# A conformer/RWKV-7 layer on one core: lora weights in buffers of their own, zero parts of tiles that persist, the first convolution tap and the bias on VectorE, and samples that write the output page

## The chip, the cores and the metric

The kernel runs on one core of a Trainium2 chip. The time is device microseconds of one execution of the whole program. Below, PE is the matrix engine (TensorE) and PEld its weight loads, DVE is VectorE, ACT is ScalarE, POOL is GpSimd and SP is the engine whose queue issues nearly all transfers. Each engine takes its instructions in the order in which they were written into its stream at build time; an instruction waits there for the semaphores of what it needs, and everything behind it on that engine waits too.

## The reference, cut to what matters

One decoder layer for 512 prompt tokens and 8 x 4 sample tokens, D_MODEL 1024, 16 heads of 64:

```
proj = h @ w_in                                        # h = rmsnorm(x)
u = u_val * sigmoid(u_gate)                            # conformer branch
c = depthwise causal conv of width 31 over u, + conv_b
o_a = silu(layer_norm(c)) @ w_conv_out
...
w_log = -softplus(-(decay_base + tanh(l_dec) @ w_decay_up)) - 0.5   # rwkv branch
a = sigmoid(iclr_base + l_iclr @ w_iclr_up)
g = sigmoid(l_gate) @ w_gate_up
step: sk = s @ kk;  s = s * w - sk (kk a)^T + v k^T;  y = s @ r
o_b = ((group_norm(y) + bonus) * g) @ w_rwkv_out
...
x = x + rms_norm((sigmoid(gA) * o_a + sigmoid(gB) * o_b) @ w_out)
x = x + rms_norm(relu(rms_norm(x) @ w_ff_up)^2 @ w_ff_down)
```

The three matrices `w_decay_up`, `w_iclr_up` and `w_gate_up` are the lora weights. The host packs them as `lora`, for each pair of heads 128 rows by 256 columns: columns 0 to 127 hold decay and iclr, 128 to 255 the gate.

## The kernel before, in words

Activations lie with channels on the partitions, and a page is 128 channels by 544 tokens (512 of the prompt, then 32 of the samples, so `T:N2` is the samples' part). Every large product is made of three matmuls on split operands (high x high, low x high, high x low) in line 152, called `lin`. A weight block of 128 x 1024 is fetched by SP (`raw`, two buffers), rounded to its high part (`whi`, line 140, on ACT or on POOL) and its low part is taken by DVE (`wlo`, line 141).

Up to about 743 us a mixing stage runs over eight pairs of heads (pairs 0 to 7 here). For pair p the loop does, in program order:

- `chain(p-1)`: the recurrence of the pair before, in eight chunks of 64 tokens, small fp32 matmuls on PE with ACT copies between (lines 655 to 686). It makes the page `y` at its fourth chunk.
- block K, then `rates(p)`: fetches the decay and iclr part of `lora` into a page of the tag `k2`, splits it into high and low (`up`), multiplies, and takes the exponentials.
- `front(p)`: scaled operands `BK` (copied by POOL, line 505) and `LR`, and the products `pb` of line 540, four chunks at a time; each group of four is copied by ACT into `nd` (line 545) and masked by DVE (`NQ`, line 547).
- `inverse(p)`: inverts the small triangular blocks. A DVE transpose into `nw` (line 575), then a loop of 15 steps of two small DVE operations each (lines 584 and 586, called the loop below), two transposes into `td` (589) and `rd` (591). Then POOL clears `DT64`, which is the first half of `nw` (594), ACT copies `td` into it (597), POOL copies `rd` into `D64` (598), and PE multiplies (line 604, `pb<-nw,NQ` first).
- `tokens(p)` (transposes into `BKt` and `SV`), `value(p)` (bonus), and `sample(p)`: the samples' recurrence. There POOL clears a strip of the state tile `st` (711) before SP fetches the state (713); at the end eight POOL instructions scale `st` (754), and SP stores it (755). The samples' output goes to a tile `yS` (745).
- `groupnorm(p-1)`: copies `yS` into `y` on ACT (760), fetches the gate part of `lora` into the page `t0` (763), splits it (`lhi` on ACT, `llo` on DVE, line 173/174), normalises and stores the page.
- `fill`: further blocks of the input projection. The convolution (`conv`, lines 285 to 307) is not run in one piece: `pump` hands out a few of its DVE steps after each block, at a lower priority. Its first tap (289) and the samples' bias (304) run on ACT, 30 taps of 128 x 512 per channel block on DVE (292).

What order the instructions of each engine finally have is set when the program is built, by a scheduler that goes by dependencies, by program order and by the priority offsets (`CP`, `HP`, `HN`), with its own estimates of durations. In each engine's stream the pieces of neighbouring pairs, of the blocks and of the convolution are therefore interleaved, and a change of one buffer can move many instructions by some places.

After the mixing stage follow the output projections, the norms and the feed-forward part, which this change does not touch.

Of the kernel before, what the change touches and what calls it, by code (L numbers as in the profile page):

```python
# [8 lines left out]
F32 = mybir.dt.float32  # L9
# [7 lines left out]
T = 512  # L17
NB = 8
TS = 4
N2 = T + NB * TS  # L20
# [42 lines left out]
def hybrid_step(ctx: ExitStack, tc: tile.TileContext, xT, hist, s0, win, wco, wro, wo, wup, wdn, lora,  # L63
# [221 lines left out]
    def conv(j, u):  # L285
# [3 lines left out]
        act(c[:, 0:T], u[:, 0:T], AF.Identity, scale=w[:, 0:1], bias=vec("conv_b", j))  # L289
# [14 lines left out]
        act(c[:, T:N2], c[:, T:N2], AF.Identity, bias=vec("conv_b", j))  # L304
# [29 lines left out]
    with ExitStack() as c1:  # L334
        P = lambda name, bufs: c1.enter_context(tc.tile_pool(name=name, bufs=bufs))
        p1 = P("p1", 1)
        p2 = P("p2", 2)
        qb = c1.enter_context(tc.tile_pool(name="qb", bufs=1, space=PSUM))
# [5 lines left out]
        D64 = p1.tile([128, NC, 64], F32, name="D64")  # L344
        MT = p1.tile([128, NC, 2, 64], F32, name="MT")
        up = [p1.tile([128, 2, 128], F32R, name=f"up{n}") for n in "hl"]
        for z in (D64, MT, *(t.bitcast(F32) for t in up)):
            nc.gpsimd.memset(z, 0.0)
# [18 lines left out]
        nc.gpsimd.memset(zbk, 0.0)  # L367
        vpad = p1.tile([128, 2, 64], F32, name="vpad")
        nc.gpsimd.memset(vpad, 0.0)

# [71 lines left out]

        def rates(p):

            lraw = page("k2")[:, 0:128]
            nc.sync.dma_start(lraw, lora[p, :, 0:128])
            yield (ACT,)
            glu_sig()
            yield
            for i in range(2):  # L450
                split_hl(up[0][H[i], i, :], up[1][H[i], i, :], lraw[H[i]])
# [39 lines left out]
        def front(p):  # L491
# [40 lines left out]
            ys[p] = p2.tile([128, N2 - T], F32, name="yS")  # L532
# [35 lines left out]
        def inverse(p, NQ, nd):  # L568
# [24 lines left out]
            DT64, xn = (nw[:, o:o + T].rearrange("p (c t) -> p c t", c=NC) for o in (0, T))  # L593
            nc.gpsimd.memset(DT64, 0.0)
# [54 lines left out]
        def chain(p, BKt, SV):  # L649

            f = fs[p]
            LR, NQ, pc = f["LR"], f["NQ"], f["pc"]
            B = (slice(0, 64), slice(64, 128))
            for c in range(NC):
# [21 lines left out]
                if c == 3:  # L676
                    if p > 1:
                        yield ("cent", p - 2)
                    y = pgs["y", p] = page("y", p2)
# [8 lines left out]
        def sample(p):  # L688
# [21 lines left out]
            sx = p1.tile([128, NB + 1, 64], F32, name="st")  # L710
            nc.gpsimd.memset(sx[:, NB, :], 0.0)
# [32 lines left out]
            for i in range(2):  # L744
                tt(out=y[H[i], :], in0=xy[0:64, 320 + 32 * i:352 + 32 * i],
                   in1=xc[0:64, 64 * i + 32:64 * i + 64], op=ADD)
# [11 lines left out]
        def groupnorm(p):  # L758
            f, y = fs[p], pgs["y", p]
            nc.scalar.copy(y[:, T:N2], ys[p])  # L760
            yc, sq = page("t0", cv), page("t1", cv)
            lraw = yc[:, 0:128]
            nc.sync.dma_start(lraw, lora[p, :, 128:256])
# [3 lines left out]
            split_hl(lhi, llo, lraw)  # L767
# [371 lines left out]
```

## Time and profile before

| | |
|---|---|
| median of 3 runs | 1330.75 us (1328.18 to 1332.06) |
| profiled execution, its own time | 1342.23 us |
| its span | 1340.4 us |
| mean granted PE clock | 0.966 |
| PE, DVE, ACT, POOL busy | 94%, 61%, 49%, 15% of the span |
| PE waits for `nw` (line 597) at line 604 | 29.8 us in 8 waits |

A row of a group reads: line, engine, operation, out<-in, count, then busy time, mean ns of one, then the engine's idle time just before these and what ended it. A row of the timeline reads: start in us, duration in us, engine, line, operation, out<-in, count, and in brackets the idle time before it and what ended that. A row of the stages gives for each stretch the busy time and number of instructions of PE, PEld, DVE, ACT and POOL, then the granted PE clock, the transfers' share and GB/s.

### The profile page before, as it was taken

What the parts mean: (1) busy time and instruction counts of PE and PEld (TensorE: products, weight loads), DVE (VectorE), ACT (ScalarE), POOL (GpSimd) and SP (SyncE); (2) the same over time, 40 slices, a digit from 0 to 9 for tenths busy, and PEclk for the clock granted to TensorE, in tenths of its full rate; (3) what the DMA queues carried; (4) which work ended last, traced back from release to release, by engine and by line L of the source; (5) the groups of instructions that cost most, each with busy time, mean ns of one, the idle gap of its engine ahead of it and who ended that gap; (6) DMA issues with size and microseconds to landing.
All of it is one profiled execution on the core that took longest, in us unless ns stands there. A gap on an engine that the chain in (4) does not pass through costs nothing.

```text
span 1340.4 us, 23228 instructions
## 1 busy us (share of the span) xinstructions
PE 1263.0 (94%) x9154; PEld 1189.1 (89%) x9154; DVE 814.7 (61%) x1529; ACT 661.2 (49%) x1587; POOL 200.2 (15%) x312
## 2 busy tenths in 40 slices
PE   7999989999898998989999999999999999999996
PEld 6988788897878888788888899999999999999995
DVE  6889878745687777878656745657633212333345
ACT  6454647555373754736434365256655222554231
POOL 1224232311333322332211100000000000000000
PEclk9999989979799898999989999999999999999998
DMA  5313121100212112120214563354022233222331
GB/s 183 105 39 100 35 90 36 65 26 26 79 34 77 34 38 71 48 86 17 66 55 145 158 239 95 93 177 128 5 82 89 79 95 96 81 93 79 95 95 67
DMA packets 46332, 110.60 MB, mean 83 GB/s; under 512 B 7184, under 2 KB 17680, under 8 KB 46224
## 3 DMA queue, kind: packets, MB, share of 16 engines
q1 hardware_dynamic: 46080, 109.05, 25.7%
q8 instruction: 72, 1.18, 0.4%
q14 instruction: 36, 0.29, 0.1%
q10 hardware_dynamic: 144, 0.07, 0.0%
HBM read 94.79 MB, written 14.32 MB: 81 GB/s over the span
## 4 chain that ended last, share of the span: by engine, by line
PE 67%; DVE 12%; ACT 11%; issue 3%; DMA 3%; POOL 3%; SPq 0%; DVEq 0%; ACTq 0%; POOLq 0%
PE lin L152 48%; PE pb L604 6%; DVE c L292 2%; ACT SV L675 2%; POOL st L754 2%; ACT SV L669 1%; DVE wlo L141 1%; PE ch L671 1%; PE yt L439 1%; PE ch L660 1%; PE ch L667 1%; PE pb L540 1%; DMA raw<-wup 1%; PE aux L720 1%; DVE R L586 1%
## 5 line engine op out<-in xcount | busy, mean ns | idle before, releaser
L152 PE MATMUL lin<-xh,whi 128*128 128x272 f32 (+1 forms) x2096 | 618.9, 296 | 3.4 <-DVE g L910 1.9
L152 PE MATMUL lin<-xl,whi 128*128 128x272 f32 (+1 forms) x2096 | 621.1, 296 | 0.3
L152 PE MATMUL lin<-xh,wlo 128*128 128x272 f32 (+1 forms) x2096 | 618.1, 295 | 0.6 <-DVE wlo L141 0.6
L152 PEld LDWEIGHTS lin<-xh,whi 128*128 128x128 f32 x2096 | 400.8, 191 | 5.7 <-DVE g L910 2.2
L152 PEld LDWEIGHTS lin<-xh,wlo 128*128 128x128 f32 x2096 | 401.3, 191 | 3.0 <-issue 1.2
L152 PEld LDWEIGHTS lin<-xl,whi 128*128 128x128 f32 x2096 | 400.8, 191 | 3.4 <-issue 1.2
L141 DVE TENSOR_TENSOR wlo<-raw,whi 128x1024 fp32r<-128x1024 f32 x131 | 160.0, 1221 | 210.1 <-ACT whi L140 172.4
L292 DVE SCALAR_TENSOR_TENSOR c<-u,cw,c 128x512 f32<-128x512 f32 x240 | 186.9, 779 | 3.9 <-DVE c L292 0.4
L140 ACT CAST whi<-raw 128x1024 fp32r<-128x1024 f32 x76 | 79.8, 1050 | 127.8 <-PE lin L152 122.0
L140 POOL CAST whi<-raw 128x1024 fp32r<-128x1024 f32 x55 | 62.2, 1130 | 302.6 <-PE lin L152 173.8
L152 PE MATMUL lin<-xh,wl 128*128 128x272 f32 x240 | 69.4, 289 | 0.0
L152 PE MATMUL lin<-xl,wh 128*128 128x272 f32 x240 | 69.3, 289 | 0.0
L152 PE MATMUL lin<-xh,wh 128*128 128x272 f32 x240 | 69.2, 288 | 0.0
L998 DVE TENSOR_TENSOR xl<-ff,xh 128x272 fp32r<-128x272 f32 x64 | 28.3, 442 | 55.9 <-ACT ff L997 55.9
L604 PE MATMUL pb<-nw,NQ 128*128 128x64 f32 x128 | 25.5, 383 | 29.8 <-ACT nw L597 29.8
L604 PEld LDWEIGHTS pb<-nw,NQ 128*128 128x128 f32 x128 | 24.3, 292 | 31.3 <-issue 31.3
L228 ACT ACT_TABLE_LOAD x37 | 47.5, 1283 | 1.8 <-PEq L1121 1.2
L675 ACT ACTIVATE SV<-ch,pc 64x64 f32<-64x64 f32 x128 | 39.5, 309 | 15.2 <-PE ch L671 13.7
L152 PEld LDWEIGHTS lin<-xh,wl 128*128 128x128 f32 x240 | 45.2, 188 | 0.1
L152 PEld LDWEIGHTS lin<-xh,wh 128*128 128x128 f32 x240 | 45.2, 188 | 0.1
L152 PEld LDWEIGHTS lin<-xl,wh 128*128 128x128 f32 x240 | 45.1, 188 | 0.1
L754 POOL TENSOR_SCALAR st<-st,epS 128x64 f32<-128x64 f32 x64 | 40.6, 657 | 11.3 <-DVE rt L584 9.5
(275 smaller groups left out, 1882.3 us busy)
## 6 DMA issues: line engine op xcount, KB each, us to landing
raw<-win SPq DMA_DIRECT2D x58, 512.0 KB, 3.7
raw<-wup SPq DMA_DIRECT2D x32, 512.0 KB, 3.6
raw<-wdn SPq DMA_DIRECT2D x32, 512.0 KB, 3.6
g_dr<-g SPq DMA_DIRECT2D x16, 272.0 KB, 2.2
raw<-wro SPq DMA_DIRECT2D x8, 512.0 KB, 3.7
raw<-wco SPq DMA_DIRECT2D x8, 512.0 KB, 3.6
raw<-wo SPq DMA_DIRECT2D x8, 512.0 KB, 3.6
x<-xT SPq DMA_DIRECT2D x8, 276.0 KB, 5.1
```

What stands on the lines that cost most here:

```text
L140: upper(hi, r)
L141: tt(out=lo, in0=r, in1=hi.bitcast(F32), op=SUB)
L152: nc.tensor.matmul(ps, a, b[:, o:o + m], start=k == 0 and i == 0, stop=k == n - 1 and i == 2)
L228: lastact[0] = nc.scalar.preload_act_table_set(name)
L292: stt(out=c[:, 0:T], in0=u[:, t:t + T], scalar=w[:, t:t + 1], in1=c[:, 0:T], op0=MULT, op1=ADD)
L439: nc.tensor.matmul(ps, lhsT, x[:, o:o + m], start=True, stop=True)
L540: nc.tensor.matmul(ps[:, c], BK[:, 4 * g + c], LR[:, 4 * g + c], start=True, stop=True)
L586: tt(out=rv, in0=rv, in1=tv, op=SUB)
L604: nc.tensor.matmul(ps[:, c, :], lhsT(c), rhs[:, c, :], start=True, stop=True)
L675: nc.scalar.mul(SV[H[i], c + 1, i, :], ch[H[i], 1, B[i]], pc[H[i], c:c + 1])
L754: nc.gpsimd.tensor_scalar(st[:, b, :], st[:, b, :], f["epS"][:, b:b + 1], None, MULT)
L998: tt(out=lo[:, q], in0=t[:, q], in1=hi[:, q].bitcast(F32), op=SUB)
```

## The change

- `lora[p]` is fetched whole (128 x 256) into a pool `p3` of two buffers. Pairs 0 and 1 are fetched ahead of the loop; pair p+1 after `groupnorm(p-1)`. `rates` and `groupnorm` read these buffers, so the two fetches per pair into `k2` and `t0` go.
- `DT64` is a tile of its own, cleared once; so is the zero strip of `st`; the two `v` tiles are made once, with their zero margins, and used in turn.
- The first convolution tap and the samples' bias are `tensor_scalar` on DVE.
- `y` is made in `front`, `sample` writes its part of it, and the copy of line 760 goes.

```
-        act(c[:, 0:T], u[:, 0:T], AF.Identity, scale=w[:, 0:1], bias=vec("conv_b", j))
+        ts(c[:, 0:T], u[:, 0:T], w[:, 0:1], vec("conv_b", j), MULT, ADD)
...
-        act(c[:, T:N2], c[:, T:N2], AF.Identity, bias=vec("conv_b", j))
+        ts(c[:, T:N2], c[:, T:N2], vec("conv_b", j), None, ADD)
...
+        p3 = P("p3", 2)
...
+        DT64 = p1.tile([128, NC, 64], F32, name="DT64")
...
-        for z in (D64, MT, *(t.bitcast(F32) for t in up)):
+        for z in (D64, DT64, MT, *(t.bitcast(F32) for t in up)):
...
+        sx = p1.tile([128, NB + 1, 64], F32, name="st")
+        nc.gpsimd.memset(sx[:, NB, :], 0.0)
...
+        vs = [p1.tile([128, 128 + T], F32, name=f"v{n}") for n in range(2)]
+        for v in vs:
+            nc.gpsimd.memset(v[:, 0:64], 0.0)
+            nc.gpsimd.memset(v[:, 64 + N2:128 + T], 0.0)
...
+        lraws = {}
+
+        def lora_in(p):
+            lraws[p] = p3.tile([128, 256], F32, name="lraw")
+            nc.sync.dma_start(lraws[p], lora[p])
+        lora_in(0)
+        lora_in(1)
+
         def rates(p):
-            lraw = page("k2")[:, 0:128]
-            nc.sync.dma_start(lraw, lora[p, :, 0:128])
-            yield (ACT,)
+            lraw = lraws[p]
             glu_sig()
-            yield
             for i in range(2):
-                split_hl(up[0][H[i], i, :], up[1][H[i], i, :], lraw[H[i]])
+                split_hl(up[0][H[i], i, :], up[1][H[i], i, :], lraw[H[i], 0:128])
...
-            ys[p] = p2.tile([128, N2 - T], F32, name="yS")
+            ys[p] = page("y", p2)
...
-            DT64, xn = (nw[:, o:o + T].rearrange("p (c t) -> p c t", c=NC) for o in (0, T))
-            nc.gpsimd.memset(DT64, 0.0)
+            xn = nw[:, T:2 * T].rearrange("p (c t) -> p c t", c=NC)
...
-                if c == 3:
-                    if p > 1:
-                        yield ("cent", p - 2)
-                    y = pgs["y", p] = page("y", p2)
...
-            sx = p1.tile([128, NB + 1, 64], F32, name="st")
-            nc.gpsimd.memset(sx[:, NB, :], 0.0)
...
-                tt(out=y[H[i], :], in0=xy[0:64, 320 + 32 * i:352 + 32 * i],
+                tt(out=y[H[i], T:N2], in0=xy[0:64, 320 + 32 * i:352 + 32 * i],
...
-            nc.scalar.copy(y[:, T:N2], ys[p])
...
-            lraw = yc[:, 0:128]
-            nc.sync.dma_start(lraw, lora[p, :, 128:256])
...
-            split_hl(lhi, llo, lraw)
+            split_hl(lhi, llo, lraws[p][:, 128:256])
...
-                v = pgs["v", p] = p2.tile([128, 128 + T], F32, name="v")
-                nc.gpsimd.memset(v[:, 0:64], 0.0)
-                nc.gpsimd.memset(v[:, 64 + N2:128 + T], 0.0)
+                v = pgs["v", p] = vs[p % 2]
...
             if p:
                 run(groupnorm(p - 1))
+                if p + 1 < NPAIR:
+                    lora_in(p + 1)
```

The streams of all engines are laid out anew. Three places of pair 5 show how; the other pairs from 3 to 6 look much the same. POOL, from the clearing of the samples' tile `uv` to the copies of `rd` into `D64`, before:

```order
L707 MEMSET uv 128x128
L140 CAST whi<-raw 128x1024
L754 TENSOR_SCALAR st<-st,epS 128x64 x8
L711 MEMSET st 128x64
L140 CAST whi<-raw 128x1024
L594 MEMSET nw 128x512
L140 CAST whi<-raw 128x1024
L598 COPY D_288<-rd 32x8x32 x4
```

The same place of POOL now:

```order
L426 MEMSET u 128x30
L715 MEMSET uv 128x128
L140 CAST whi<-raw 128x1024
L760 TENSOR_SCALAR st<-st,epS 128x64 x8
L140 CAST whi<-raw 128x1024 x2
L610 COPY D_291<-rd 32x8x32 x4
```

The two clearings between the scaling of `st` and the weight casts are gone, and the casts follow the scaling directly.

ACT just ahead of the copies of `td` that the first product of line 604 needs, before:

```order
L760 COPY y<-yS 128x32
L289 ACTIVATE c<-u,vt,cw 128x512
L411 COPY gsg<-lin 128x272 x2
L235 ACTIVATE gsg<-gsg 128x544
L663 COPY xs<-ch 128x128
L173 CAST lhi<-t_6006 128x128
L378 ACTIVATE k<-lin,vt 128x276
L304 ACTIVATE c<-c,vt 128x32
L597 COPY nw<-td 32x8x32 x4
```

The same place of ACT now:

```order
L173 CAST lhi<-lraw 128x128
L419 COPY gsg<-lin 128x272 x2
L235 ACTIVATE gsg<-gsg 128x544
L675 COPY xs<-ch 128x128
L386 ACTIVATE k<-lin,vt 128x276
L609 COPY DT_292<-td 32x8x32 x4
```

The first tap, the bias and the copy of `yS` are gone from ACT, and the cast of the gate lora weights stands earlier.

DVE in the last steps of the loop, from a low part `wlo` to the transpose into `td`, before (`rt` and `R` are the loop's own operations, `k` the evacuation of the next pair's block K):

```order
L141 TENSOR_TENSOR wlo<-raw,whi 128x1024
L586 TENSOR_TENSOR R<-R,rt 128x2x4x3
L174 TENSOR_TENSOR llo<-t_6006,lhi 128x128
L584 TENSOR_TENSOR rt<-R,nw 128x16
L292 SCALAR_TENSOR_TENSOR c<-u,cw,c 128x512
L586 TENSOR_TENSOR R<-R,rt 128x2x4x2
L301 TENSOR_REDUCE c<-cx 128x16
L584 TENSOR_TENSOR rt<-R,nw 128x8
L292 SCALAR_TENSOR_TENSOR c<-u,cw,c 128x512
L586 TENSOR_TENSOR R<-R,rt 128x2x4
L379 SCALAR_TENSOR_TENSOR k<-lin,omu,k 128x276
L589 STREAM_TRANSPOSE td<-R 128x8x8x4
```

DVE now, from some steps earlier in the loop on, where `llo` has moved to and where the first tap stands:

```order
L141 TENSOR_TENSOR wlo<-raw,whi 128x1024
L599 TENSOR_TENSOR R<-R,rt 128x2x3x7
L174 TENSOR_TENSOR llo<-lraw,lhi 128x128
L597 TENSOR_TENSOR rt<-R,nw 128x36
L289 TENSOR_SCALAR c<-u,cw,vt 128x512
L599 TENSOR_TENSOR R<-R,rt 128x2x3x6
L299 TENSOR_TENSOR cx<-u,cw 128x496
L597 TENSOR_TENSOR rt<-R,nw 128x30
L292 SCALAR_TENSOR_TENSOR c<-u,cw,c 128x512
```

`llo` stands one weight block earlier in the loop, and the first tap has become one more large DVE operation inside it; the loop of this pair still has two `wlo` and five taps.

More of the change, by code (lines that the diff above doesn't have):

```diff
@@ L651, in chain @@
             f = fs[p]
-            LR, NQ, pc = f["LR"], f["NQ"], f["pc"]
+            LR, NQ, pc, y = f["LR"], f["NQ"], f["pc"], ys[p]
             B = (slice(0, 64), slice(64, 128))
@@ L758, in groupnorm @@
         def groupnorm(p):
-            f, y = fs[p], pgs["y", p]
-            nc.scalar.copy(y[:, T:N2], ys[p])
+            f, y = fs[p], ys[p]
             yc, sq = page("t0", cv), page("t1", cv)
-            lraw = yc[:, 0:128]
-            nc.sync.dma_start(lraw, lora[p, :, 128:256])
             lhi = p1.tile([128, 128], F32R, name="lhi")
```

## The prediction

> **What bounds the kernel now.** I read first the stages before and after the end of the mixing (and 100 us of the feed-forward part), then the waits of PE, longest first. A stage's row gives its length, the busy time and number of instructions of PE, PEld, DVE, ACT and POOL, and then the granted clock.
>
> ```profile
> 0.00:743.00 743.00, 684.85 (x4613) 614.61 (x4613) 554.73 (x1093) 400.16 (x1093) 195.09 (x308) 0.95 0.21 68
> 743.00:1340.00 597.00, 578.12 (x4541) 574.53 (x4541) 259.98 (x437) 261.09 (x495) 5.10 (x4) 0.99 0.32 101
> 1000.00:1100.00 100.00, 100.00 (x800) 100.00 (x799) 26.57 (x30) 36.87 (x66) 0.00 (x0) 1.00 0.27 86
> PE pb L604 <- ACT nw L597: 29.8, 8, 6.0
> PE aux L169 <- DVE acc L878: 3.5, 2, 2.1
> ```
>
> PE is the bound in both stages. The second is untouched and nearly full; the 100 us in it give the step of a weight matmul, 100/800 = 0.125 us. In the mixing stage PE is idle for 743 - 684.85 = 58 us, and one wait makes half of that: the first product of the inverse waits for ACT's copies of `td`, once per pair.
>
> ```profile
> 124.05 0.29 PE L604 MATMUL pb<-nw,NQ 128*128 128x64 f32 x1 [0.56 <-ACT nw L597]
> 193.62 0.29 PE L604 MATMUL pb<-nw,NQ 128*128 128x64 f32 x1 [3.72 <-ACT nw L597]
> 263.35 0.29 PE L604 MATMUL pb<-nw,NQ 128*128 128x64 f32 x1 [1.52 <-ACT nw L597]
> 356.26 0.45 PE L604 MATMUL pb<-nw,NQ 128*128 128x64 f32 x1 [5.44 <-ACT nw L597]
> 437.40 0.44 PE L604 MATMUL pb<-nw,NQ 128*128 128x64 f32 x1 [6.02 <-ACT nw L597]
> 516.10 0.44 PE L604 MATMUL pb<-nw,NQ 128*128 128x64 f32 x1 [5.07 <-ACT nw L597]
> 597.33 0.45 PE L604 MATMUL pb<-nw,NQ 128*128 128x64 f32 x1 [5.30 <-ACT nw L597]
> 675.34 0.44 PE L604 MATMUL pb<-nw,NQ 128*128 128x64 f32 x1 [2.14 <-ACT nw L597]
> ```
>
> These are pairs 0 to 7. ACT is not slow there: it waits for `td`, which ends DVE's loop. PE's weight matmuls cover the loop, and what the loop lasts beyond them is the wait. Each wait has a second price, read from the stages behind it (the last number but two is the granted clock):
>
> ```profile
> 193.97:200.80 6.83, 6.83 (x34) 6.83 (x33) 3.22 (x5) 3.01 (x7) 2.73 (x4) 0.50 0.22 59
> 265.65:286.13 20.48, 20.27 (x91) 19.74 (x90) 6.45 (x8) 6.62 (x16) 1.04 (x1) 0.50 0.09 29
> 354.39:368.04 13.65, 11.78 (x52) 11.70 (x53) 8.14 (x11) 6.20 (x13) 3.28 (x4) 0.50 0.13 40
> 675.25:682.08 6.83, 6.74 (x31) 6.77 (x32) 0.44 (x1) 1.16 (x2) 0.51 (x2) 0.50 0.15 58
> 911.00:918.00 7.00, 6.25 (x48) 6.17 (x49) 4.47 (x12) 4.66 (x10) 0.00 (x0) 1.00 0.45 156
> ```
>
> Pair 1 and pair 7 are the first and the last of five stretches of 6.83 us at half clock (pairs 1, 4, 5, 6, 7); pair 2 has 20.48 us, pair 3 13.65. Pair 0 with its 0.56 us has none. So a wait of 1.52 us or more was followed by half clock seven times of seven, and a stretch of 6.83 us costs 6.83/2 = 3.4 us of PE. Once it was not so: the 2.1 us for `acc` end at 912 us at full clock. Between 1.5 and 2.1 us I take it as even.
>
> **What prolongs the loop.** DVE's own rows inside it:
>
> ```profile
> 345.42 1.23 DVE L141 TENSOR_TENSOR wlo<-raw,whi 128x1024 fp32r<-128x1024 f32 x1 [4.62 <-POOL whi L140]
> 427.27 1.23 DVE L141 TENSOR_TENSOR wlo<-raw,whi 128x1024 fp32r<-128x1024 f32 x1 [2.91 <-POOL whi L140]
> 429.82 0.29 DVE L174 TENSOR_TENSOR llo<-t,lhi 128x128 fp32r<-128x128 f32 x1 [1.23 <-ACT lhi L173]
> 507.17 1.23 DVE L141 TENSOR_TENSOR wlo<-raw,whi 128x1024 fp32r<-128x1024 f32 x1 [1.64 <-POOL whi L140]
> 510.07 0.29 DVE L174 TENSOR_TENSOR llo<-t,lhi 128x128 fp32r<-128x128 f32 x1 [1.59 <-ACT lhi L173]
> 587.35 1.23 DVE L141 TENSOR_TENSOR wlo<-raw,whi 128x1024 fp32r<-128x1024 f32 x1 [2.08 <-POOL whi L140]
> 590.28 0.29 DVE L174 TENSOR_TENSOR llo<-t,lhi 128x128 fp32r<-128x128 f32 x1 [1.61 <-ACT lhi L173]
> 180.63 1.23 DVE L141 TENSOR_TENSOR wlo<-raw,whi 128x1024 fp32r<-128x1024 f32 x1 [2.67 <-POOL whi L140]
> 344.24 0.15 POOL L711 MEMSET st<- 128x64 f32 x1 [2.38 <-DMA wkvs<-st]
> 426.09 0.15 POOL L711 MEMSET st<- 128x64 f32 x1 [2.93 <-DMA wkvs<-st]
> 673.35 0.30 ACT L173 CAST lhi<-t 128x128 fp32r<-128x128 f32 x1 [2.23 <-DMA t<-lora]
> ```
>
> DVE waits for a weight cast of POOL, which stands behind the clearing of `st`; that clearing waits for the store of the pair before. POOL's rows in pairs 5 and 6 read alike. Then DVE waits for `llo`, whose high part waits for the lora fetch.
>
> **The change, part by part.** *Clearing of `st` gone.* The cast follows the scaling directly, so pair 3 gains the 2.38 us of the store's wait, and pairs 4, 5, 6 their whole DVE waits of 2.91, 1.64, 2.08 (the store's wait is no shorter). Pair 1 gains nothing: its cast waits for the scaling itself. SP's fetch of the next state still waits for the store, with weight fetches behind it; two `raw` buffers cover that.
>
> *Lora prefetch.* The waits of 1.23, 1.59, 1.61 go, and in pair 7, where ACT had the cast of 673.35 just ahead of the copies, some 0.9: the copies could have followed `td` 0.9 us sooner. Two fetches per pair on SP become one. Its buffer is free when `llo` of two pairs ago is read, so this fetch can hold up the weight fetch behind it until then; in the order `llo` now stands one weight block earlier, and I cost it at nothing under the two `raw` buffers. Uncovered it would be one late cast, as in pair 1, 2.7 us.
>
> *Clearing of `DT64`, `v` gone; `y` written directly.* Off the path: PE waits for `td`, and POOL's clearing is done before. Zero, with the few tenths between `td` and the copies as the most to win.
>
> *Reordering.* From the order I count what stands inside each loop (DVE), and the matmuls of line 152 between the last product of line 540 and the first of 604 (PE's cover), at these rows, in the first five with groups of instructions as on the page, then two of the chain of waits:
>
> ```profile
> L292 DVE SCALAR_TENSOR_TENSOR c<-u,cw,c 128x512 f32<-128x512 f32 x240 | 186.9, 779 | 3.9 <-DVE c L292 0.4
> L299 DVE TENSOR_TENSOR cx<-u,cw 128x496 f32<-128x496 f32 x16 | 11.4, 715 | 0.0
> L301 DVE TENSOR_REDUCE c<-cx 128x16 f32<-128x496 f32 x16 | 10.5, 656 | 0.0
> L100 DVE TENSOR_SCALAR nvt<-vt 128x138 f32<-128x138 f32 x1 | 0.7, 725 | 0.0
> L289 ACT ACTIVATE c<-u,vt,cw 128x512 f32<-128x512 f32 x8 | 6.5, 816 | 35.8 <-DVE u L424 35.8
> 241.16 0.66 PE ch L632 x4
> 242.04 1.69 PE aux L720 x16
> 190.90 0.49 DVE L379 SCALAR_TENSOR_TENSOR k<-lin,omu,k 128x276 f32<-128x276 f32 x1
> 242.45 0.59 ACT L633 COPY BKt<-ch 128x512 f32<-128x512 f32 x1
> ```
>
> The first tap on DVE has no row. It has one large input where the reduction and the other taps have one and two, so it lies between 0.66 and 0.78 us, or lower if DVE is faster with scalars alone; I take 0.65, and the bias, 32 columns, at nothing. A tap is 0.75 from start to start.
>
> Pair 0: three taps fewer, a first tap, a `cx` and a reduction more, -0.25; cover 199 to 193 matmuls, -0.8; together +0.55. Pair 1: -0.1 and cover -0.2, +0.1. Pair 2: `llo` and an evacuation of `k` come in, +0.8; cover the same. Pair 3: a third `wlo` and a first tap, +1.9; cover +14 matmuls (1.75), but the eight state products of line 720 (1.69) have moved ahead of it, -0.1; together +2.0. Pair 4: a tap and a first tap more, a reduction fewer, +0.75; nine matmuls fewer (1.1) and three small products of the chain more, for which I take 0.65 after the 0.66 of four transposes, -0.45; +1.2. Pair 5: a first tap, +0.65; five matmuls more, eight transposes of line 632 moved ahead (twice 0.66 less their overlap), -0.3; +0.95. Pair 6: two taps fewer, a first tap, -0.85; six matmuls fewer, -0.8; 0. Pair 7: `llo`, +0.3, cover -0.3; +0.6. In sum +6.2 us. In pairs 2 and 5 the copy into `BKt` that stood between the copies into `nd` now stands ahead of them, -0.6 each.
>
> *Start.* POOL clears one tile of 128x512 and the margins more, and SP issues two fetches ahead of two weight fetches. The chain shows PE in weight matmuls without a gap at that time, so nothing:
>
> ```profile
> 29.05 16.43 PE lin L152 x128
> ```
>
> **The sum.** The waits become: pair 0 1.1; pair 1 3.8; pair 2 1.52 + 0.8 - 0.6 = 1.7; pair 3 5.44 + 2.0 - 2.4 = 5.0; pair 4 6.02 + 1.2 - 4.1 = 3.1; pair 5 5.07 + 0.95 - 3.2 - 0.6 = 2.2; pair 6 5.30 - 3.7 = 1.6; pair 7 2.14 + 0.6 - 0.9 = 1.8. That is 20.3 instead of 29.8, a gain of 9.5 us. Of the stretches at half clock those of pairs 2, 5, 6 and 7 come to the doubtful length; two of four gone are 6.8 us. Against the profiled execution: 1342.2 - 9.5 - 6.8 = 1326, and less 10.2 for the excess over 6.83 us in pairs 2 and 3, (13.65 + 6.82)/2, which I take for this execution's own: it is nearly all of the 11.5 us by which it lies above the median of 1330.75. From the median, whose runs I take to have 6.83 us each: 1330.75 - 16.3 = 1314 us. What is late next: in pairs 1 and 3 POOL's scaling of `st`, ahead of the cast.
>
> **The rivals.** *The clock forgives more.* If half clock needs a longer wait than the rows suggest, only pairs 1 and 3 keep it: five stretches gone, 17 us, and 1330.75 - 9.5 - 17 = 1304. For it speaks the wait at 912 us, against it pairs 2 and 7 (1.52 and 2.14 us). [...]
>
> *DVE's loop is the limit (slower).* The waits on POOL and ACT are only where DVE's lateness shows: the cast then waits for what it needs itself, as it mostly does:
>
> ```profile
> POOL whi L140 <- PE lin L152: 173.8, 23, 26.0
> ```
>
> Then the 14.4 us of stalls and the 1.2 of `BKt` come back elsewhere, and the +6.2 us inside the loops remain: 1337. It decides from where less than 2.2 of these 15.6 us go (the net must be worse by 4.0). Against it: DVE's waits in pairs 3 and 4 both end 1.03 us after the clearing ends (345.42 and 427.27 against 344.24 + 0.15 and 426.09 + 0.15), one cast's length, so there it is the clearing that sets them.
>
> *It doesn't do what it says.* The casts start earlier but about as much as the order takes back: 6.2 to 10.2 of the 15.6 us go, no stretch of half clock is lost, and the time is 1327 to 1334.7. For it: the scheduler places the product by its own estimate, and has erred by 5 us in four pairs.
>
> **How the numbers follow.** A difference of 0.3%, 4.0 us, is about what a measurement of this kernel can tell from none. The forecast, gains of 8 to 23 us: 0.66. The clock's rival: 0.12. No effect: 0.13. DVE the limit: 0.09. Faster is the first two, 0.78; same 0.13; slower 0.09. The range's low end is 1297: the added 6.2 us turn out hidden and the clock's rival holds. Its high end is 1329: half of the 15.6 us go (7.8 - 6.2 = 1.6 us), with all stretches at half clock kept.
>
> **What would show it.** Right: no POOL wait for the store and no ACT wait for lora; DVE's waits for `whi` in pairs 4 to 6 near zero, in pair 1 still over 2 us; PE's waits at the first product near 20 us, the longest in pairs 1 and 3; stretches at half clock gone behind waits under 1.5 us. Wrong: a new wait of DVE in the loop (for the first tap's buffer, or a weight fetch behind the lora fetch), PE's products placed earlier, or a stretch at half clock where no wait stands.

## The result, and the profile after

The changed kernel took 1312.33 us in the median of 4 runs (1311.47 to 1317.42) beside 1331.4 us for the kernel before: a ratio of 0.9864, 95% interval 0.9821 to 0.9907. Timed again it took 1312.86 us in the median of 5 runs, ratio 0.984 (0.981 to 0.987). The profiled execution took 1317.42 us itself.

First the stages of the profiled execution, as in the prediction, and two rows of its waits (total, number, longest):

```profile
0.00:743.00 743.00, 694.38 (x4776) 619.39 (x4777) 577.93 (x1131) 400.92 (x1088) 188.57 (x285) 0.97 0.22 72
743.00:1315.00 572.00, 554.66 (x4380) 551.98 (x4379) 242.40 (x415) 251.37 (x476) 1.04 (x1) 0.99 0.32 100
PE pb L616 <- ACT DT L609: 14.0, 8, 4.4
ACT lhi L173 <- PE yt L152: 21.7, 6, 7.5
```

In the first 743 us PE issues 163 matmuls more than before and is idle for 48.6 us instead of 58. The wait at the first product of `inverse` is 14.0 us instead of 29.8. ACT's cast of the lora weights no longer waits for a transfer, and no row of POOL waiting for the store is left. The eight waits, pairs 0 to 7, in the timeline of PE:

```profile
126.93 0.55 PE L616 MATMUL pb<-DT,NQ 128*128 128x64 f32 x3 [0.41 <-ACT DT L609]
198.09 0.69 PE L616 MATMUL pb<-DT,NQ 128*128 128x64 f32 x2 [4.42 <-ACT DT L609]
268.77 0.55 PE L616 MATMUL pb<-DT,NQ 128*128 128x64 f32 x3 [0.70 <-ACT DT L609]
349.34 0.43 PE L616 MATMUL pb<-DT,NQ 128*128 128x64 f32 x2 [0.31 <-ACT DT L609]
420.56 0.69 PE L616 MATMUL pb<-DT,NQ 128*128 128x64 f32 x2 [4.27 <-ACT DT L609]
497.73 0.43 PE L616 MATMUL pb<-DT,NQ 128*128 128x64 f32 x2 [1.25 <-ACT DT L609]
574.30 0.55 PE L616 MATMUL pb<-DT,NQ 128*128 128x64 f32 x3 [1.28 <-ACT DT L609]
654.90 0.55 PE L616 MATMUL pb<-DT,NQ 128*128 128x64 f32 x3 [1.36 <-ACT DT L609]
```

Two long ones are left, in pairs 1 and 4. Behind both stands the same thing, shown here on DVE (both pairs) and on POOL (pair 4):

```profile
183.90 1.23 DVE L141 TENSOR_TENSOR wlo<-raw,whi 128x1024 fp32r<-128x1024 f32 x1 [2.59 <-POOL whi L140]
406.54 1.23 DVE L141 TENSOR_TENSOR wlo<-raw,whi 128x1024 fp32r<-128x1024 f32 x1 [2.74 <-POOL whi L140]
402.19 3.34 POOL L760 TENSOR_SCALAR st<-st,epS 128x64 f32<-128x64 f32 x8 [1.74 <-DVE rt L597]
405.47 1.04 POOL L140 CAST whi<-raw 128x1024 fp32r<-128x1024 f32 x1
```

POOL's eight scalings of `st` take 3.34 us, and the cast for which DVE waits comes after them. What stands at half clock near the first products is now (stages, granted clock the last number but two):

```profile
197.43:204.26 6.83, 6.17 (x28) 6.17 (x29) 4.53 (x6) 4.18 (x11) 3.24 (x4) 0.50 0.26 79
419.29:426.12 6.83, 5.56 (x25) 5.56 (x26) 4.26 (x8) 4.16 (x11) 2.01 (x4) 0.50 0.28 73
504.63:508.04 3.41, 3.41 (x18) 3.41 (x17) 2.30 (x4) 0.78 (x2) 0.00 (x0) 0.50 0.00 0
576.31:586.55 10.24, 9.36 (x43) 9.07 (x42) 4.11 (x6) 1.47 (x3) 1.50 (x2) 0.50 0.15 51
```

Pairs 2, 3 and 7 have none any more. Pair 6 has one behind its wait of 1.28 us, and pair 5 one behind a second wait, that of its second product:

```profile
502.56 0.63 PE L616 MATMUL pb<-D,MT 128*128 128x64 f32 x4 [1.38 <-issue]
```

**Waits and clock as two accounts.** Each run lists its span and mean granted clock. At half clock a microsecond does about half the work: over the profiles a product of line 152 of 128x272 starts every 0.125 us at full clock and every 0.227 us at half (medians). So (1 - clock) times the span is about the time that the clock cost (some 10% too much, by these two numbers), and the rest is about the time of the same instructions and waits at full clock. For 29 runs of the kernel before, from 1326.5 to 1345.8 us, the rest is 1296.9 us with a deviation of 1.4: nearly all of the spread between runs of one kernel is clock. Means over the runs:

| kernel (runs) | median us | mean clock | clock's cost us | rest us |
|---|---|---|---|---|
| before (29) | 1333.04 | 0.9722 | 37.1 | 1296.9 |
| `st_alone` (12) | 1326.53 | 0.9766 | 31.1 | 1297.0 |
| `lora_alone` (6) | 1322.88 | 0.9752 | 32.9 | 1290.8 |
| `tap_alone` (12) | 1337.36 | 0.9703 | 39.7 | 1298.1 |
| `clr_alone` (12) | 1328.03 | 0.9747 | 33.6 | 1293.2 |
| `zeros_alone` (7) | 1322.06 | 0.9784 | 28.6 | 1294.9 |
| `after_again` (5) | 1312.86 | 0.9826 | 22.8 | 1290.0 |
| `clearing_back` (6) | 1319.43 | 0.9805 | 25.7 | 1294.0 |
| `no_tap` (5) | 1311.07 | 0.9826 | 22.8 | 1288.1 |
| `scale_on_dve` (6) | 1307.91 | 0.9817 | 24.0 | 1286.0 |
| `no_tap_scale_on_dve` (6) | 1305.16 | 0.9847 | 20.0 | 1284.0 |

The kernel before was timed anew beside each group of kernels: 1333.0 us beside the first four parts, 1335.1 beside `after_again`, `no_tap` and `scale_on_dve`, 1331.6 beside `clearing_back` and the last version, 1331.0 beside `zeros_alone`. Ratios below are against the one timed beside. Its rest was 1296.2 to 1297.0 each time, but its clock's cost was 37.1, 37.5, 35.0 and 34.0 us, so clock costs of different groups compare only to some 3 us. The whole change is 6 to 7 us of rest and 14 us of clock.

### The profile page after: what moved, and what is told of

Read it like the earlier page. It is cut to its first block, busy times and chain, and to the rows that moved or that the text cites. A ratio compares the mean times of both kernels' runs of the same rounds, so it can differ in the third digit from the quotient of the medians.

```text
span 1315.6 us, 23135 instructions
## 1 busy us (share of the span) xinstructions
PE 1249.0 (95%) x9154; PEld 1171.4 (89%) x9154; DVE 820.3 (62%) x1545; ACT 652.3 (50%) x1563; POOL 189.6 (14%) x286
## 4 chain that ended last, share of the span: by engine, by line
PE 65%; DVE 16%; ACT 12%; issue 3%; DMA 2%; POOL 1%; SPq 0%; DVEq 0%; ACTq 0%; POOLq 0%
PE lin L152 46%; PE pb L616 5%; DVE c L292 3%; ACT SV L687 2%; DVE wlo L141 2%; ACT SV L681 2%; DVE R L599 1%; PE ch L683 1%; PE ch L672 1%; PE yt L447 1%; PE ch L679 1%; PE aux L447 1%; DVE rt L597 1%; PE pb L553 1%; DMA raw<-wo 1%
## 5 line engine op out<-in xcount | busy, mean ns | idle before, releaser
L292 DVE SCALAR_TENSOR_TENSOR c<-u,cw,c 128x512 f32<-128x512 f32 x240 | 189.6, 790 | 5.8 <-issue 1.3
L140 POOL CAST whi<-raw 128x1024 fp32r<-128x1024 f32 x55 | 65.0, 1181 | 327.1 <-PE lin L152 181.5
L681 ACT ACTIVATE SV<-ch 64x64 f32<-64x64 f32 x128 | 27.7, 217 | 34.1 <-PE ch L679 32.2
L998 ACT ACTIVATE ff<-lin 128x272 f32<-128x272 f32 x64 | 25.2, 394 | 29.7 <-PE lin L152 29.6
L760 POOL TENSOR_SCALAR st<-st,epS 128x64 f32<-128x64 f32 x64 | 36.1, 605 | 10.7 <-DVE rt L597 9.0
```

The costliest lines, as they stand in the source:

```text
L140: upper(hi, r)
L292: stt(out=c[:, 0:T], in0=u[:, t:t + T], scalar=w[:, t:t + 1], in1=c[:, 0:T], op0=MULT, op1=ADD)
L681: nc.scalar.mul(SV[H[i], c, i, :], ch[H[i], 2, B[i]], -1.0)
L760: nc.gpsimd.tensor_scalar(st[:, b, :], st[:, b, :], f["epS"][:, b:b + 1], None, MULT)
L998: act(t[:, q], ps, AF.Relu)
```

## The experiments

**Four parts alone.** Each is the kernel before with one part of the change.

```diff
 st_alone: made once, beside the other constants
+        sx = p1.tile([128, NB + 1, 64], F32, name="st")
+        nc.gpsimd.memset(sx[:, NB, :], 0.0)
 ... (the same two lines leave sample)
```

> The kernel before, with one edit: the tile of the sample states (`sx`) is made once and its zero strip cleared once. The order on PE and DVE around the inverse is word for word that of the kernel before. Theory A (stalls of the loop and the clock, as predicted): DVE's waits for the `whi` cast fall by 2.38 us in pair 3 and vanish in pairs 4, 5, 6 (2.91, 1.64, 2.08), PE's waits at the first product become about 3.1, 3.1, 3.4, 3.2 there (8 waits, 20.8 us in all instead of 29.8), still long enough for half clock behind each, so the time is 1331 - 9 = 1322, and it lies between 1318 and 1325. Theory B (the lora fetch takes the place of it): `llo` waits longer by what `wlo` waits less in pairs 4 to 6, only pair 3 gains, 1329. Theory C (the gain of the whole change came from the other order of instructions, not from stalls taken away): 1331, since the order is unchanged.

Ratio 0.9957 (0.9934 to 0.998). The time of 1326.5 us lies between the theories; the waits show theory B. DVE's waits for the cast are gone in pairs 4, 5 and 6 as expected, and its waits for `llo`, one or two instructions later, have grown from 1.23, 1.59 and 1.61 to:

```profile
416.23 0.29 DVE L174 TENSOR_TENSOR llo<-t,lhi 128x128 fp32r<-128x128 f32 x1 [4.35 <-ACT lhi L173]
497.66 0.29 DVE L174 TENSOR_TENSOR llo<-t,lhi 128x128 fp32r<-128x128 f32 x1 [2.63 <-ACT lhi L173]
579.33 0.29 DVE L174 TENSOR_TENSOR llo<-t,lhi 128x128 fp32r<-128x128 f32 x1 [3.78 <-ACT lhi L173]
415.90 0.30 ACT L173 CAST lhi<-t 128x128 fp32r<-128x128 f32 x1 [6.35 <-DMA t<-lora]
PE pb L606 <- ACT nw L599: 30.6, 8, 6.7
```

The last but one row is why: the lora transfer lands when it lands. Over pairs 3 to 6 the loop's waits for the cast fell by 9.2 us and those for `llo` rose by 8.0. PE waits 30.6 us in all, no less than before, and the rest is 1297.0 against 1296.9. Still the kernel is faster, by clock alone. Why the clock is better at equal waits is not settled.

```diff
 lora_alone
+        p3 = P("p3", 2)
+            lraws[p] = p3.tile([128, 256], F32, name="lraw")
+            nc.sync.dma_start(lraws[p], lora[p])
 ... (two fetches per pair gone; the next fetch is issued after groupnorm)
```

> The kernel before, with one edit: the lora weights have their own buffers and are fetched one pair ahead in one transfer. The order on DVE and PE changes a little. Theory A: DVE's waits for `llo` in pairs 4, 5, 6 (1.23, 1.59, 1.61) and ACT's wait for the transfer in pair 7 (0.9 of 2.23) go, while the waits for the `whi` cast stay (4.6, 2.9, 1.6, 2.1 in pairs 3 to 6); PE's waits at the first product sum to about 25 us instead of 29.8, and the time is 1331 - 5 = 1326 (1323 to 1329). Theory B: the clearing of `st`, which still waits for the store, now sets the loop's end alone, and nothing is gained: 1331. Theory C: the gain of the whole change came from the other order; this edit moves the order, so it would show a gain of up to 19 us.

Ratio 0.9928 (0.9904 to 0.9952), 9.6 us: more than theory A gave, and the largest of the four. DVE's waits for POOL's casts stay in sum (31.7 us before), those of PE fall by 8.3 us:

```profile
PE pb L610 <- ACT nw L603: 21.5, 8, 4.6
DVE wlo L141 <- POOL whi L140: 33.1, 20, 3.7
```

This edit also moves the order: PE's cover in pair 4 is 140 matmuls of line 152 instead of 154, and the wait of pair 2 grows from 1.52 to 3.58 us while that of pair 4 falls from 6.02 to 2.53. How much of the 9.6 us is the order's was not separated.

```diff
 tap_alone
-        act(c[:, 0:T], u[:, 0:T], AF.Identity, scale=w[:, 0:1], bias=vec("conv_b", j))
+        ts(c[:, 0:T], u[:, 0:T], w[:, 0:1], vec("conv_b", j), MULT, ADD)
-        act(c[:, T:N2], c[:, T:N2], AF.Identity, bias=vec("conv_b", j))
+        ts(c[:, T:N2], c[:, T:N2], vec("conv_b", j), None, ADD)
```

> The kernel before, with one edit: the first convolution tap and the bias on VectorE instead of ScalarE. The first tap adds 8 x 0.54 us to DVE. Theory A: all stalls for POOL and for the lora transfer stay; the loops of pairs 3 and 6 hold one first tap more (pair 6 also a third `wlo`, under a cover that is 29 weight matmuls longer), pair 4 a cover 16 matmuls shorter with two taps more (about +3.5 us of wait). Sum within 3 us of none: 1331, 1327 to 1335. Theory B: ScalarE was late for the convolution (it waited 35.8 us for `u`), and taking the tap from it frees its queue for the copies of `td`: a gain of 4 us or more. Theory C: the other order alone brings the whole gain, and this edit, which moves most of it, comes near 1312.

Ratio 1.0036 (1.0014 to 1.0057): slower by 4.8 us. Theory B is out, and so is C, since this edit moves the order and does not gain. Theory A's range of 3 us either way is passed too. Of the price 1.2 us is rest and 2.6 clock, by the means of the table.

```diff
 clr_alone
+        DT64 = p1.tile([128, NC, 64], F32, name="DT64")     (cleared once)
-            nc.gpsimd.memset(DT64, 0.0)
 ... (v's margins cleared once; y made in front, written by sample directly)
```

> The kernel before, with two edits that the prediction cost at nothing: `DT64` and the margins of `v` are cleared once and persist, and the samples write their outputs straight into the page `y`. The order around the inverse is that of the kernel before. Theory A: nothing on the path, 1331 within 1.5 us, and the delay from `td` to its first copy falls from 0.1 to 1.0 us to under 0.1 in each pair. Theory B: those delays were on the path, and their sum of some 3 us over the eight pairs comes off: 1328.

> The kernel before, with only `DT64` and the margins of `v` cleared once; the samples still write into a tile of their own and ScalarE copies it. The order around the inverse is that of the kernel before. It tells apart what in the pair of edits `clr_alone` gained 7.2 us where the prediction had none. Theory A (the copies of `td` into `nw` waited for POOL's clearing: 0.45 us in pair 2, 0.34 and 0.25 in pairs 3 and 4, and each copy and each first product started 0.06 to 0.1 us later than with the tile of its own; together 2.5 us, doubled by the clock): all of it, 1326 to 1329 beside 1333. Theory B (it came from the page `y`, which takes a copy from ScalarE and changes its order in pair 7, where the high part of the lora weights stood ahead of the copies): 1331 or more, and pair 7 keeps its delay of 1 us.

The pair of edits gave 0.9946 (0.992 to 0.9973), the zeros without the page `y` 0.994 (0.9918 to 0.9963): the zeros bring it, `y` nothing that shows. These gains, 7 to 8 us, are above the theories' (some 3 us for the pair, 4 to 7 for the zeros). Before, ACT's copies in pair 2 could start only when POOL had cleared their target. Pair 2 on POOL, on DVE and ACT, and then on ACT with the zeros alone:

```profile
261.01 0.52 POOL L594 MEMSET nw<- 128x512 f32 x1
260.66 0.45 DVE L589 STREAM_TRANSPOSE td<-R 128x256 f32<-128x256 f32 x1
261.56 1.64 ACT L597 COPY nw<-td 32x256 f32<-32x256 f32 x4 [1.60 <-POOL nw L594]
262.28 1.65 ACT L601 COPY DT<-td 32x256 f32<-32x256 f32 x4 [1.18 <-DVE td L594]
```

`td` ended at 261.11, the clearing at 261.53; in the other pairs the clearing was done before `td`. With the tile of its own the copies follow `td` after 0.03 us in six pairs (0.09 in four of them before), and the first product follows the copies after 0.05 us instead of 0.14. In pairs 3 and 4 the delays of 0.34 and 0.25 us stay, in the runs of both edits; in pair 3 ACT is still in an activation of 0.75 us when `td` ends. Pair 7 gained its 0.94 us in another way, and here the order is not that of the kernel before: ACT's cast of the lora weights, which stood ahead of the copies, stands behind them. ACT in pair 7 with the zeros alone, then with the lora edit alone:

```profile
665.75 1.64 ACT L601 COPY DT<-td 32x256 f32<-32x256 f32 x4 [1.52 <-DVE td L594]
667.42 0.30 ACT L173 CAST lhi<-t 128x128 fp32r<-128x128 f32 x1
655.33 1.65 ACT L603 COPY nw<-td 32x256 f32<-32x256 f32 x4 [1.52 <-POOL nw L600]
```

With the lora edit alone the copies are still 0.92 us late there, because POOL's clearing, behind a cast, then comes last. PE's waits at the first product fall by 2.4 us with the zeros (27.4 instead of 29.8), about as much as the rest; the remainder of the gain is clock.

By the ratios the four parts make -5.7, -9.6, +4.8 and -7.2 us, together -17.7; the whole change made -18 to -21. They add up within their intervals, which are some 3 us either way for each part.

**The same change again, and the kernel before again.**

> The changed kernel again, unchanged, beside the other kernels of this call. The runs so far say that the spread of one kernel's times is that of its granted clock: for the kernel before, time less (1 - clock) x span is 1296.9 with a deviation of 1.4, while the time itself runs from 1326 to 1346. Theory A (stalls and clock): the changed kernel's time less its clock part is 1290 (6.5 us of stalls gone), its clock is about 0.982 instead of 0.972 (the remaining 13 us), in all 1312 to 1315. Theory B (the gain was mostly clock by chance of the first few runs): the clock is 0.975 to 0.978 here, and the time 1318 to 1322.

> The kernel before, unchanged, for one more profile: the one on record lay 11.5 us above the median of its runs, with stretches at half clock of 20.5 and 13.7 us in pairs 2 and 3. Theory A (the length of these two was that execution's own, as the prediction took it): stretches of 3.4 to 6.8 us there, all in all some 61 us of half clock in the span less its last 12 us instead of 80, a mean clock of 0.970 to 0.975 and a time of 1330 to 1336, with the same waits of PE at the first product within 0.3 us in each pair. Theory B: the same stretches again, and a time near 1342.

The changed kernel repeats, in rest (1290.0) and in clock (0.9826): theory A. Its profile's span is 3.0 us shorter than that of the first one (1312.6 against 1315.6), and 2.4 of them are one wait at 886 us, 4.29 there and 1.89 here. The kernel before, profiled again at 1333.64 us, has the same waits within 0.3 us but in pair 6 (5.9 instead of 5.3) and other stretches:

```profile
263.40:266.81 3.41, 3.41 (x17) 3.41 (x17) 0.29 (x1) 2.46 (x7) 1.53 (x3) 0.50 0.35 101
345.32:358.97 13.65, 11.10 (x51) 11.13 (x52) 8.32 (x13) 6.07 (x13) 3.27 (x4) 0.50 0.12 40
505.75:519.40 13.65, 12.00 (x55) 12.03 (x56) 7.98 (x11) 5.69 (x14) 3.30 (x4) 0.50 0.12 39
```

Pair 2's 20.48 us are 3.41 here; pair 3's 13.65 came again, and pair 5 has 13.65 too. Theory A holds for pair 2 and falls for pair 3. So of the 10.2 us that the prediction took for its profile's own, pair 3's part was not. In sum without the last 12 us of the span: 81.9 us at half clock in the first profile of before, 68.3 in this one, 41.0 in both profiles of the changed kernel.

**Waits of chosen length.** Into the quiet stage of the changed kernel:

```diff
+            src = part[j][:, N2 - 64:N2]
+            for _ in range(IDLE[half][j]):          # 0 to 18 copies
+                z = fp.tile([128, 64], F32, name="zi", tag="zi", bufs=2)
+                ts(z, src, 1.0, None, MULT)
+                src = z
+            stop = nc.tensor.matmul(zp[:, 0:64], ident, src, start=True, stop=True)
 ... (the next block's matmuls are issued behind stop)
```

> The changed kernel with waits of chosen length put into its quiet part: after each of 12 blocks of 96 weight matmuls of the feed-forward part (`down`), a chain of 0 to 18 small VectorE copies starts from the block's evacuation, a 128x64 product of PE reads its end, and the next block is issued behind that product. So PE idles by itself for about 0.8 + 0.2 us per copy, 0.8 to 4.5 us, between stretches of full work of 12 us. Nothing is left out. Theory W (from the traces of the single edits: all stretches at half clock start on one fixed grid of 3.413 us, and the clock of a window goes by the idle time in the window before): a stretch starts only on that grid; it follows where one window held over 1.9 us of idle, never where it held under 1.0; an idle of 2.5 us or more is then nearly always followed by half clock, one of 1.2 to 2.2 us sometimes, by where it lies in the grid; lengths are multiples of 3.41 us. Theory P (the prediction's): every idle over 2.1 us is followed by 6.83 us, none under 1.5. [...] The time is that of the changed kernel plus the idles (25 to 28 us) plus half of the stretches: 6 to 17 us by W, 20 by P, 7 by S.

Five of the twelve waits, in the timeline of PE, and stages around some of them:

```profile
1034.16 0.43 PE L1060 MATMUL aux<-zi,cs 128*128 128x64 f32 x2 [2.60 <-DVE zi L1057]
1106.36 0.66 PE L1060 MATMUL aux<-zi,cs 128*128 128x64 f32 x2 [5.21 <-DVE zi L1057]
1264.94 0.41 PE L1060 MATMUL aux<-zi,cs 128*128 128x64 f32 x2 [1.31 <-DVE zi L1057]
1280.56 0.41 PE L1060 MATMUL aux<-zi,cs 128*128 128x64 f32 x2 [3.13 <-DVE zi L1057]
1317.64 0.66 PE L1060 MATMUL aux<-zi,cs 128*128 128x64 f32 x2 [5.45 <-DVE zi L1057]
1032.31:1035.72 3.41, 1.56 (x12) 1.57 (x13) 1.52 (x3) 0.48 (x2) 0.00 (x0) 1.00 0.57 169
1035.72:1039.13 3.41, 3.41 (x17) 3.41 (x16) 0.00 (x0) 0.00 (x0) 0.00 (x0) 0.50 0.28 111
1039.13:1042.55 3.42, 3.42 (x29) 3.42 (x29) 0.00 (x0) 0.30 (x1) 0.00 (x0) 1.00 0.00 0
1103.99:1110.82 6.83, 4.46 (x20) 4.49 (x21) 1.92 (x10) 0.00 (x0) 0.00 (x0) 0.50 0.26 77
1264.00:1281.48 17.48, 13.41 (x105) 13.25 (x106) 7.09 (x17) 3.81 (x6) 0.00 (x0) 1.00 0.33 98
```

A step is one interval of 3.413 us of the grid on which the stretches start. In the first three stages a step with the wait of 2.60 in it is followed by one at half clock and then full clock again; the last stage holds a wait of 1.31 us and, at its end, that of 3.13, and its clock is full throughout. The waits came out at 0.85 to 6.36 us, 41 us in sum instead of the 25 to 28 expected, so the time passed every theory's sum and only the stretches tell the theories apart. The three of 0.85, 1.29 and 1.31 have no half clock behind them. The six of 2.60 to 4.30 have one stretch of 3.41 us each, the three of 5.21, 5.45 and 6.36 one of 6.83 each. By S only the two longest chains, of 13 and 18 copies, would be followed by half clock. It is out: 2.60 us suffice, behind two copies and in a step in which PE was busy for 1.56 of 3.41 us. Theory P is out as to length. Theory W holds: the first six stretches start at 1035.72, 1052.79, 1069.85, 1086.92, 1103.99 and 1124.47 us, which are 5, 5, 5, 5 and 6 steps of 3.413 apart. The time is 1373.2, 60.3 above the changed kernel; by the waits (twelve, 41 us) and half of the twelve steps (20.5) it should be 61.

**The clearing put back**, the only edit taken from the changed kernel:

```diff
 clearing_back (in sample)
+            sx = p1.tile([128, NB + 1, 64], F32, name="st")
+            nc.gpsimd.memset(sx[:, NB, :], 0.0)
```

> The changed kernel with one edit taken back: the tile `sx` is made in each sample step and its zero strip cleared by POOL again. The order of all engines around the inverse is word for word that of the changed kernel. Theory A (without the lora waits behind it, the clearing's wait for the store is on the path): POOL waits for the store 2 to 3 us in pairs 3 to 7 again, DVE's wait for the `whi` cast rises from 2.74 to about 5 us in pair 4 and from nothing to 1.5 to 2 in pairs 3, 5 and 6, PE's waits at the first product go from 14 to about 23 us; with the clock the time is 1313 + 9 + 3 to 7 = 1325 to 1329. Theory B (the loops have room, as the single edit, whose gain was in the clock alone, suggests): PE's waits rise by less than 3 us, and the time stays under 1317.

Ratio 0.9907 (0.987 to 0.9943), 1319.43 us: 6.6 above the changed kernel, between the theories. PE's waits at the first product are 16.8 us in sum, 2.8 more than in the changed kernel, which is theory B's count. On PE pairs 5 and 6, on POOL pair 5, on DVE pair 4:

```profile
501.52 1.10 PE L614 MATMUL pb<-DT,NQ 128*128 128x64 f32 x8 [2.89 <-ACT DT L607]
579.00 0.69 PE L614 MATMUL pb<-DT,NQ 128*128 128x64 f32 x2 [3.46 <-ACT DT L607]
493.20 0.15 POOL L717 MEMSET st<- 128x64 f32 x1 [2.60 <-DMA wkvs<-st]
493.31 1.04 POOL L140 CAST whi<-raw 128x1024 fp32r<-128x1024 f32 x1
405.91 1.23 DVE L141 TENSOR_TENSOR wlo<-raw,whi 128x1024 fp32r<-128x1024 f32 x1 [2.75 <-POOL whi L140]
```

In pairs 5 and 6 the wait comes back as expected, 1.6 and 2.2 us. In pair 3 DVE waits 1.82 us again and PE's wait stays 0.3 under its longer cover. In pair 4 nothing changes: there the cast for which DVE waits follows the scaling directly, and the clearing stands behind that cast. So the edit that alone took nothing off the rest is worth 4.0 us of it (1294.0 against 1290.0) beside the rest of the change.

**Two versions further on.**

```diff
 no_tap: the change without the two ts(...) lines of tap_alone
 scale_on_dve: the change, and in sample
-            for b in range(NB):
-                nc.gpsimd.tensor_scalar(st[:, b, :], st[:, b, :], f["epS"][:, b:b + 1], None, MULT)
+            tt(out=st, in0=st, in1=f["epS"].unsqueeze(2).to_broadcast([128, NB, 64]), op=MULT)
```

> All of the change but the first tap and the bias, which stay on ScalarE. Theory A (the edits add up: alone, the tap cost 4.8 us, the three others gained 5.7, 9.6 and 7.2): 1333 - 22 = 1311, that is 2 to 5 us faster than the whole change beside it. Theory B (the tap costs 8 x 0.54 us on DVE only where it stands in a loop that PE waits for, and its order happened to be a bad one when alone): equal to the whole change within 2 us. Theory C (ScalarE's relief is needed once the other stalls are gone): slower than the whole change by 3 us or more. In all three DVE's waits for the `llo` part and POOL's for the store stay away.

> The changed kernel, with the eight POOL scalings of `st` (128x64 each) replaced by one VectorE multiplication of 128x512. Theory A (late next is POOL's scaling ahead of the cast): DVE's waits for the `whi` cast of 2.59 us in pair 1 and 2.74 us in pair 4 go, PE's waits at the first product there fall from 4.4 and 4.3 to about 2, with at most one stretch at half clock left of the two, at 0.75 us of DVE per pair more; the time is 5 us below the changed kernel beside it (3 to 9). Theory B (the cast then waits for its own data, the wait comes back as one for `raw` or for the weights' buffers): equal within 2 us.

> Both further versions together: the first tap and the bias stay on ScalarE, and the scaling of `st` is one VectorE multiplication. Theory A (the gains add): 1.8 us from the tap and 5 us from the scaling, 1306 beside 1313 for the changed kernel. Theory B (the order decides: without the tap it puts the cast far enough behind the scaling in most pairs, so that the scaling on VectorE only adds its 0.75 us per loop): 1309 to 1312, no better than the scaling with the tap (1308).

Without the tap: 0.9826 (0.9795 to 0.9856), 1.8 us below the change beside it. The ratios do not separate them; the rest does, 1288.1 against 1290.0, with deviations of 0.6 and 1.1 in five runs each. That is nearest to B, and C is out: ScalarE needed no relief. What `no_tap` gains is not in the waits at the first product, which are 16.6 us there; where it lies was not worked out. With the scaling on VectorE: 0.9824 (0.9787 to 0.986), 5 us below in the median (2.8 in the mean, since its clock cost 1.2 us more), 4.0 in rest: theory A. DVE's waits for the cast in the loops of pairs 1 and 4 are gone, and PE's waits there are 1.53 and 1.06 us. Both: 0.9782 (0.974 to 0.9824), 1305.16 us, below both kernels, and theory A again. Its row of waits:

```profile
PE pb L616 <- ACT DT L609: 10.4, 8, 1.9
```

Eight waits of at most 1.9 us are left of the 29.8.

## Why the prediction was right, and where it was not

The forecast of 1314 us (1297 to 1329) met 1312.3 and 1312.9. Its mechanism held: stalls of DVE's loop, seen by PE as one wait per pair, and half clock behind it. That the sum came out so near is luck, since its errors cancel: 15.8 us of waits gone instead of 9.5, some 9 us given back instead of none, and 14 us of clock instead of 6.8.

- *The stalls of the store and the lora transfer go.* Right; both kinds of row are gone. What the prediction did not see is that they stand in series on DVE: with the clearing alone gone, 8.0 of 9.2 us came back as waits for `llo`, while beside the rest of the change the same edit is worth 4.0 us of rest. That it is the lora edit which frees them is read from the rows; no run has these two edits and nothing else. Pair 7's 0.9 us was set down to the lora fetch, but it stayed with the lora edit alone (0.92) and went with the zeros alone.
- *The waits: 20.3 us in sum.* 14.0. The mis-sized terms are pair 3 (5.0; 0.31) and pair 4 (3.1; 4.27), both in the step that says which cast follows POOL's scaling: "in pairs 1 and 3" was to be late next, and it is pairs 1 and 4. The order moved the scaling away from DVE's next cast in pair 3, where the whole wait of 4.62 us went and not 2.38 of it, and up to it in pair 4. Pair 3's cover also grew, from 28.9 to 30.8 us where -0.1 was set; 1.25 us of that is other idle time of PE inside it. Pairs 5 and 6 are 1.25 and 1.28 instead of 2.2 and 1.6, pair 7 1.36 instead of 1.8, pair 2 0.70 instead of 1.7; pair 1 4.42 instead of 3.8.
- *"Clearing of `DT64`, `v` gone: zero ... POOL's clearing is done before."* Wrong. In the profile before, pair 2's row of ACT names POOL as its releaser. Alone it is worth 7 to 8 us, 2 to 4 of them rest; of the 2.4 us of PE's waits, 0.4 is that clearing, 0.9 the new order in pair 7, and the remainder the copies and products that start some 0.1 us sooner in each pair.
- *The first tap: 0.65 us, the bias nothing.* The rows after:

```profile
L289 DVE TENSOR_SCALAR c<-u,cw,vt 128x512 f32<-128x512 f32 x8 | 5.4, 670 | 0.0
L304 DVE TENSOR_SCALAR c<-c,vt 128x32 f32<-128x32 f32 x8 | 2.3, 284 | 0.0
76.81 0.36 PE L152 MATMUL lin<-xh,whi 128*128 128x272 f32 x1 [2.05 <-DVE r L394]
```

0.67 and 0.28 us (mean of eight). The tap's mean is as estimated, but by one of 1.27 us; the median is 0.54. The bias is 2.3 us of DVE in sum where nothing was set. The third row is a wait of PE in pair 0 that was 0.76 us before and is 1.69 with the tap alone; `no_tap` has 1.63 there for another input, so it is not the tap's alone.
- *Nothing is given back elsewhere* (the sum has no such term). Wrong by some 9 us. PE's time from start to start, above the lower quartile of the same line and shape, divides like this (worked out from the start times of all 9154 matmuls, second profile of each kernel):

```
us above the quartile            before    after
gap before the first products      32.0     15.3
within stretches at half clock     29.2     17.9
other gaps over 0.5 us             20.3     24.3
other gaps of 0.15 to 0.5 us       66.2     70.2
below 0.15 us                      64.0     65.2
```

  16.7 us are gone at the first products, 9.2 are back in smaller gaps. By the first profiles 2.2 us of this are two waits of pair 0 (0.76 and 1.81 us before, 2.05 and 2.70 after). That PE meets more small waits because it runs closer to DVE and ACT is a likely reading, and was not tried.
- *The clock: two stretches of 6.83 us, 6.8 us.* It was 14, by the mean clocks (37.1 to 22.8) and by the stretches of the second profiles, (68.3 - 41.0)/2 = 13.7. The prediction's seven stretches of 6.83 us, with the four of 3.41 us elsewhere in its profile, make 61 us before and 48 after; 68.3 and 41.0 were measured, so each end was off by 7.
- *A wait of 1.5 us or more is followed by half clock; between 1.5 and 2.1 even.* Wrong in form, as the stretches behind 1.28 and 1.38 us show: in the profiles, at full clock, half clock followed the idle time within one step of the grid of 3.413 us, always above 1.87 us and never below 1.0 (below). The 7 us by theory S, in the sum for the waits of chosen length, count on half clock behind the two longest waits alone, which no run shows: a wait of 2.60 us was followed by a stretch of 3.41.
- *Rivals.* The clock forgives more: no, pairs 5 and 6 lost clock at waits of under 1.4 us, and in the quiet stage a wait of 2.60 us was enough. DVE's loop is the limit: no, though PE gets 9 us of small waits back; the loops of pairs 5 and 6 fell from 25.6 to 22.7 and from 27.1 to 22.5 us. Doesn't do what it says: no, the stalls' rows are gone and the time at half clock fell from 68.3 to 41.0 us.

## What to carry to other kernels

Two stalls in series on one engine hid each other here, 8.0 of 9.2 us: ask of each what the engine would wait for next. Removing the first alone can show nothing in the waits (`st_alone`), so it is judged together with the second. Where PE is the bound, split a gain into time at full clock and clock by the runs' mean clocks before explaining it; here the clock was two thirds of it, 14 us of 20 to 21. A scaling of 3.34 us on POOL cost here what stood behind it in that engine's queue, a cast for which DVE waited 2.74 us, so a clearing or scaling there is looked up by the cast that follows it, and after each re-ordering anew.

## What the runs showed of the hardware

- In the clock records of the 14 profiles all 129 stretches at half clock start on one grid of 3.413 us through the whole execution, within 3 ns of their profile's. Those of before and after, but for the one at the end of each span, last one to six steps, 3.41 to 20.48 us. The following count takes the 5145 steps at full clock from 5 us on, without the last 12 us of each span. All 95 that held more than 1.87 us of idle PE were followed by half clock, none of the 4934 that held less than 1.0, and 33 of the 116 between. In `idle_lengths` a step in which PE was busy for 1.56 of 3.41 us was followed by half clock.
- In `idle_lengths` a wait of 2.60 to 4.30 us in dense work cost one step, 1.7 us on top of itself. Behind the first products of `inverse` it was one to six steps, the six (20.48 us) behind a wait of 1.52 us that had one step behind it in the second profile. PE's idle time does not explain this: of 213 steps at half clock, 98 were followed by another, 38 of these with under 0.05 us of idle PE in them. What keeps the clock low there is not settled; the small products of 64 columns that follow were not tried by themselves.
- The grid's place in the span differs from one execution to the next, so that a wait need not fall at the same place in the grid: the stretch of pair 2 starts at 265.65 us in the first profile of before and at 263.40 in the second, that of pair 1 at 193.97 and 191.72, both 2.25 us apart. With the rest constant to 1.4 us, this would explain a spread of 19 us between runs of one kernel; that it is the cause was argued from the two accounts, not tried.
- One VectorE multiplication of 128x512 with a broadcast operand took 0.68 us, eight POOL instructions of 128x64 for the same work 3.34 us in pair 4 and 5.09 in pair 5.
